# Token-major projections with 512 (in the first mixer 416) weight columns to a matmul, over four PSUM banks

## The chip, the cores and the metric

The kernel runs on one core of a Trainium2 chip. The metric is the device time of one execution in microseconds (us). It computes in float32; its large products are made of three matmuls each, on float32 values split into two halves of a narrower format (float32r).

## The reference

The input is a sequence of 512 tokens of width 1024 and a memory of 256 tokens. A first block has two layers (mixer, attention to the memory, squared-ReLU MLP); a second block has two hybrid layers with a context of 256 tokens. What the change touches are the projections whose result is wanted with tokens on the partitions:

```python
# first mixer: 512 columns for pooling, then latents of queries (256), keys and values (128), rotary keys (32)
u = h @ w_in_e[e]
b = mla_mixer(u[..., o1:o2], u[..., o2:o3], u[..., o3:], ...)
# second mixer: 16 heads of 64
qkv = (h @ w_qkv_o[o]).reshape(B, S, 3, NA_HEADS, NA_HEAD_DIM)
q = rms_norm(qkv[:, :, 0], na_q_g[o])
k = rms_norm(qkv[:, :, 1], na_k_g[o])
c = neighbourhood_attention(q, k, qkv[:, :, 2], na_rpb[o])
...
# hybrid layers: both for the 512 latents and the 256 tokens of context
# parts: ret q, k, v, gate (512 each), gla q, k (256 each), gla v, gate (512 each), two gate ranks of 16
lat = jnp.split(h @ w_in, offsets, axis=-1)
r = bidirectional_scan(retention_inputs(lat, True), ...)   # 4 heads, values of 128
g = bidirectional_scan(gla_inputs(lat), ...)               # 4 heads, values of 128
ret = from_heads(head_layernorm(r)) * jax.nn.silu(parts[3])
gla = from_heads(rmsnorm(g, gla_norm_g)) * jax.nn.silu(parts[7])
return jnp.concatenate([ret, gla], axis=-1) @ w_out
```

The second hybrid layer needs no output of the context, and so has no gates for it.

## The kernel before, in words

Activations lie feature-major in SBUF, 128 features by 512 tokens to a tile, as pairs `hi`, `lo`. Weights come from HBM in chunks of 512 KB on the SyncE queue (SP); `wload` (lines 227 to 244) casts a chunk to `whi` on ACT (line 241) and subtracts for `wlo` on DVE (line 242). All matmuls are issued on line 159 (`mat`), three to a product (`mat3`: hi by hi, hi by lo, lo by hi), and all transposes on line 171.

Most products are feature-major (`linear`): weights are the stationary operand, and 512 tokens stream by. Some are token-major (`linear_tm`, line 298): 128 tokens are the stationary operand and the weight columns stream by, 256 of them here. The result of 128 tokens by 256 columns is half of a PSUM bank, so a bank holds two token tiles (`per = 2`); 512 tokens need two banks and the context's 256 tokens one. An `evac` function, called once a bank at the product's end, copies the bank to SBUF on ACT.

There are eight banks in four sets: three `mm` for large products, three `pt` for transposes, scores and small products, one `po` for attention outputs, and one `bank` for streams that run beside the main one (the memory's keys and values, the modulation vectors). A bank that is given back can be written again when its last reader has read it.

The program is written by streams (generators). `run` (line 208) always steps the first stream whose operands should be there, by a clock that sums the length of the matmuls written so far; a stream yields how long its operands take or a condition. `take` and `give` (lines 174 and 181) count the banks that a stream holds over several steps. So each engine has a fixed queue, in which the pieces of many streams alternate, and the evacuations are written with `high_priority(200)`, which moves them forward in their engine's order.

The token-major products are: in the first mixer the latents, 256 and 160 columns after one another (`evac_c`, line 619: copies with a scale on ACT, lines 626 and 628, and squares); in the second mixer, for each of four groups of four heads, queries, keys and values of 256 columns each (`project`, line 873; `tm` is a copy of two token tiles, line 885, that is then normalized); in the hybrid layers `values` and `gates` (lines 1192 and 1203) with two products of 256 columns each, for keys "g" (gated heads) and "r" (retention heads). `values` copies a bank to `v` on ACT (line 1196). `gates` copies it to `gate_in` (line 1207), and then makes x sigmoid(x) of it: Abs, Exp, Ln, a DVE step, Exp on ACT, and a product on GpSimd (lines 1208 to 1213).

Beside these run the heads. A gated head (`gla`, line 1369) begins with a small matmul of its gates (tiles `gup` and `dd` or `dup` into `pt`), then a chain over ACT and DVE: Abs, Exp, Ln (lines 1375 to 1377, into `gb`), a scan and sums on DVE (`gc`, `tot`), Exp into `et` and `gb`, Exp into `ei` and `gc` (lines 1389 to 1397), then transposes of `gb` (to `ke`) and products of `gc` and `ei`. Two heads of a kind are under way at a time. `finish` (line 1269) normalizes a head's output and multiplies the gate. In the second mixer a `unit` (line 934) is the attention of two heads for 128 queries: scores in `pt`, Exp into `P` (line 957), two transposes, a copy `PT` (lines 969 and 972), products into `po`. In a hybrid layer the order of the projections is: gate ranks, gla keys, values "g", gla queries, ret keys, values "r", ret queries, gates "g", gates "r"; the products of the output follow.

Of the kernel before, what the change touches and what calls it, by code (L numbers as in the profile page):

```python
# [14 lines left out]
ALU = mybir.AluOpType  # L15
# [40 lines left out]
class Half:  # L56
    """a half of the tokens of a list of pairs of tiles, which may grow"""
# [24 lines left out]
class Net:  # L82
# [21 lines left out]
    # ---- storage  # L104
# [50 lines left out]
    # ---- tensor engine  # L155
# [17 lines left out]
    # ---- banks that a stream holds over several of its steps  # L173
# [52 lines left out]
    # ---- weights: a chunk of up to 1024 columns as an exact sum of two float32r tiles  # L226
    def wload(self, src, a, b, cut=1):
        nc = self.nc
        if self.side:
# [68 lines left out]
    def linear_tm(self, w, k0, kn, c0, cn, xs, ntok, evac, cut=1):  # L298
        """Token-major: 128 tokens on partitions; evac(i, tile of tokens i and features c0...)."""
# [4 lines left out]
        yield from self.take("mm", n // per)  # L304
        ps = [self.mm((128, per, cn)) for _ in range(n // per)]
        for kb in range(0, nk, kc):
            if len(xs) < kb + kc:
                yield lambda: len(xs) >= kb + kc
            hi, lo = self.wload(w[k0 + kb * 128:k0 + (kb + kc) * 128, c0:c0 + cn], kc, cn, cut if kb == 0 else 1)
# [5 lines left out]
            if kb + kc == nk:  # L315
# [3 lines left out]
                self.give("mm", n // per)  # L319
# [19 lines left out]
    def rows(self, r, n, copy=True):  # L339
        """a value of every token (tokens on partitions, column i for tile i), on all partitions"""  # L340
# [12 lines left out]
    def sq_add(self, st, x, w=T, half=None):  # L353
        """adds x * x to the running tile in the list st, or to a half of it"""
# [22 lines left out]
    def pair(self, w, nm=("hi", "lo")):  # L377
        """room for the two halves of w columns"""
# [12 lines left out]
    def split(self, x, g=None, w=T, rows=128, pair=None):  # L391
        """x (times a column g) as an exact sum of two float32r tiles"""
# [10 lines left out]
    # ---- residual stream  # L403
# [35 lines left out]
    # ---- keys and values of the memory  # L439
    def memory(self):  # L440
# [29 lines left out]
        for s in range(4):  # L470
# [6 lines left out]
            yield from self.linear_tm(A["w_mem_kv"], 0, D, D + s * 256, 256, h, NMEM, evac_v)  # L477
# [76 lines left out]
    # ---- squared-ReLU MLP of the first block  # L554
# [32 lines left out]
    # ---- first mixer: pooling and latent attention  # L587
    def mixer0(self):
# [30 lines left out]
        def evac_c(parts, dst):  # L619
            def f(q, p):  # L620
                w = parts[-1][1]
                c = self.t2(nm="c", w=2 * w).rearrange("p (i c) -> p i c", i=2)
                junk = self.t2(nm="junk", w=w)
                for ii in range(2):
                    i = q * 2 + ii
# [1095 lines left out]
```

## Time and profile before

| | us |
|---|---|
| median of 3 runs | 3344.96 (3344.82 to 3346.26) |
| profiled execution, span from first to last instruction | 3351.3 |
| TensorE (PE) busy | 3268.7, 98% |
| DVE busy | 1784.2, 53% |
| ACT busy | 1204.7, 36% |
| GpSimd (POOL) busy | 207.9, 6% |

The profile page gives one execution. Its span is the only time that it has for that execution, and it is 6.3 us over the median of the runs. PE is TensorE's matmuls, PEld its weight loads, which overlap them. The granted clock is the share of TensorE's full speed that it was given; its mean over the span is 0.986. In a row of the trace, `out<-in` are the program's tiles without their numbers, and what stands in brackets at its end is the idle time of the engine before it and what ended it.

The stages follow one another like this: first mixer and memory to about 190 us, modulation, memory attention and MLP to 880, second mixer to about 1133, its output, memory attention and MLP to 1633, hybrid layer 0 to 2080 and its MLP to 2600, hybrid layer 1 to 2990 and its MLP to the end.

### The profile page before, as it was taken

What the parts mean: (1) busy time and instruction counts of PE and PEld (TensorE: products, weight loads), DVE (VectorE), ACT (ScalarE), POOL (GpSimd) and SP (SyncE); (2) the same over time, 40 slices, a digit from 0 to 9 for tenths busy, and PEclk for the clock granted to TensorE, in tenths of its full rate; (3) what the DMA queues carried; (4) which work ended last, traced back from release to release, by engine and by line L of the source; (5) the groups of instructions that cost most, each with busy time, mean ns of one, the idle gap of its engine ahead of it and who ended that gap; (6) DMA issues with size and microseconds to landing.
All of it is one profiled execution on the core that took longest, in us unless ns stands there. A gap on an engine that the chain in (4) does not pass through costs nothing.

```text
span 3351.3 us, 45020 instructions
## 1 busy us (share of the span) xinstructions
PE 3268.7 (98%) x17942; PEld 2675.4 (80%) x17942; DVE 1784.2 (53%) x3208; ACT 1204.7 (36%) x2157; POOL 207.9 (6%) x257
## 2 busy tenths in 40 slices
PE   8999999999999999999999999999999989899998
PEld 8745448888988778888888987888888879788887
DVE  6853126444555646444776587333334755774444
ACT  5732224222444443222553354221322533433323
POOL 0100000000011100000011212000000011200000
PEclk9999999999999999999999999999999999899999
DMA  5356542332322123333442321222221433123332
GB/s 154 119 165 213 190 149 89 98 97 95 117 60 85 63 67 94 96 99 95 135 121 76 89 83 59 68 63 63 63 63 59 122 89 88 51 64 98 97 94 76
DMA packets 301858, 323.99 MB, mean 97 GB/s; under 512 B 18832, under 2 KB 270608, under 8 KB 301648
## 3 DMA queue, kind: packets, MB, share of 16 engines
q1 hardware_dynamic: 296656, 315.22, 30.9%
q10 hardware_dynamic: 4992, 5.90, 0.6%
q8 instruction: 141, 2.31, 0.3%
q14 instruction: 69, 0.57, 0.1%
HBM read 310.05 MB, written 2.10 MB: 93 GB/s over the span
## 4 chain that ended last, share of the span: by engine, by line
PE 93%; DVE 4%; ACT 1%; DMA 1%; issue 1%; SPq 0%; ACTq 0%; DVEq 0%
PE mm L159 77%; PE pt L159 6%; PE po L159 4%; PE bank L1023 3%; PE pt L171 1%; PE bank L159 1%; DMA raw<-in_w_mem_kv 1%; DVE wlo L242 1%; PE mm L171 0%; DVE S L1444 0%; DVE ht L1057 0%; ACT whi L241 0%; DVE sq L360 0%; DVE o L1289 0%; DMA raw<-in_w_in_e 0%
## 5 line engine op out<-in xcount | busy, mean ns | idle before, releaser
L242 DVE TENSOR_TENSOR wlo<-raw,whi 128x1024 fp32r<-128x1024 f32 (+2 forms) x503 | 598.1, 1190 | 747.5 <-ACT whi L241 724.6
L241 ACT CAST whi<-raw 128x1024 fp32r<-128x1024 f32 (+2 forms) x503 | 504.4, 1005 | 1248.4 <-PE mm L159 1094.4
L159 PE MATMUL mm<-hi,whi 128*128 128x512 f32 (+2 forms) x2768 | 887.1, 358 | 15.4 <-DVE cx L1124 6.1
L159 PE MATMUL mm<-hi,wlo 128*128 128x512 f32 (+2 forms) x2288 | 842.2, 369 | 0.0
L159 PE MATMUL mm<-lo,whi 128*128 128x512 f32 (+2 forms) x1808 | 707.7, 392 | 1.7 <-DVE lo L1062 1.6
L159 PEld LDWEIGHTS mm<-hi,whi 128*128 128x128 f32 (+1 forms) x2768 | 493.9, 190 | 111.3 <-issue 25.0
L159 PEld LDWEIGHTS mm<-hi,wlo 128*128 128x128 f32 (+1 forms) x2288 | 433.4, 189 | 85.8 <-issue 17.0
L159 PE MATMUL mm<-ahi,whi 128*128 128x512 f32 (+1 forms) x1552 | 489.7, 352 | 0.0
L159 PE MATMUL mm<-ahi,wlo 128*128 128x512 f32 (+1 forms) x1296 | 471.8, 366 | 0.0
L159 PEld LDWEIGHTS mm<-lo,whi 128*128 128x128 f32 (+1 forms) x1808 | 340.8, 188 | 87.4 <-issue 17.5
L159 PE MATMUL mm<-alo,whi 128*128 128x512 f32 (+1 forms) x1040 | 399.6, 386 | 0.0
L159 PE MATMUL mm<-whi,hi 128*128 128x256 f32 (+2 forms) x1392 | 367.5, 291 | 17.4 <-ACT v L1196 7.6
L159 PE MATMUL mm<-wlo,hi 128*128 128x256 f32 (+2 forms) x1200 | 346.3, 289 | 2.1 <-DVE wlo L242 2.1
L159 PEld LDWEIGHTS mm<-ahi,whi 128*128 128x128 f32 x1552 | 277.4, 189 | 40.8
L159 PE MATMUL mm<-whi,lo 128*128 128x256 f32 (+2 forms) x1008 | 289.4, 289 | 0.6 <-DVE lo L400 0.6
L159 PEld LDWEIGHTS mm<-whi,hi 128*128 128x128 f32 x1392 | 258.3, 195 | 25.3 <-ACT v L1196 7.8
L159 PEld LDWEIGHTS mm<-ahi,wlo 128*128 128x128 f32 x1296 | 244.4, 189 | 39.4
L159 PEld LDWEIGHTS mm<-wlo,hi 128*128 128x128 f32 x1200 | 234.4, 196 | 10.4 <-issue 6.4
L159 PEld LDWEIGHTS mm<-alo,whi 128*128 128x128 f32 x1040 | 195.5, 188 | 38.3
L159 PEld LDWEIGHTS mm<-whi,lo 128*128 128x128 f32 x1008 | 195.9, 195 | 5.5 <-issue 4.8
L1124 DVE SCALAR_TENSOR_TENSOR x<-mm,mod,x 128x512 f32<-128x512 f32 (+1 forms) x102 | 72.2, 717 | 99.5 <-PE mm L159 99.2
L1023 PE MATMUL bank<-ada,sil 128*32 128x512 f32 x384 | 122.4, 602 | 0.9 <-DMA ada<-in_ada_w 0.9
(320 smaller groups left out, 3254.4 us busy)
## 6 DMA issues: line engine op xcount, KB each, us to landing
raw<-in_w_ff SPq DMA_DIRECT2D x128, 512.0 KB, 3.6
raw<-in_w_mlp SPq DMA_DIRECT2D x128, 512.0 KB, 3.6
raw<-in_w_in SPq DMA_DIRECT2D x98, 512.0 KB, 3.8
ada<-in_ada_w SPq DMA_DIRECT2D x192, 256.0 KB, 3.7
raw<-in_w_qkv SPq DMA_DIRECT2D x24, 512.0 KB, 3.6
raw<-in_w_out SPq DMA_DIRECT2D x24, 512.0 KB, 3.5
raw<-in_w_mem_kv SPq DMA_DIRECT2D x32, 256.0 KB, 3.8
raw<-in_w_mem_q SPq DMA_DIRECT2D x16, 512.0 KB, 3.5
```

The lines of the kernel that those rows point to most:

```text
L159: return self.nc.tensor.matmul(out, lhsT=lhsT, rhs=rhs, start=start, stop=stop, **k).ins
L171: self.nc.tensor.transpose(out, in_, self.ident)
L241: nc.scalar.copy(hi[:, v], raw[:, v])
L242: nc.vector.tensor_sub(lo[:, v], raw[:, v], f32(hi[:, v]))
L1023: nc.tensor.matmul(p[32 * g:32 * g + 32], lhsT=sil[:, k], rhs=w, start=(k == 0), stop=(k == KT - 1), tile_position=(0, 32 * g))
L1124: self.nc.vector.scalar_tensor_tensor(x, p, self.mod[l][:, 16 + 24 * j + m, st:st + 1], x, ALU.mult, ALU.add)
```

## The change

`linear_tm` takes any number of column slices; with more than 256 columns a token tile has a bank of its own (`per = 1`), so 512 tokens take three `mm` banks and a fourth, which is `po` in the first mixer and the single `bank` elsewhere. All are held until the product's end. `wload` gets a list of slices, with a DMA for each. Docstrings and comments are taken out as well, which moves the line numbers (the cast of a chunk from 241 to 246, the copy `v` from 1196 to 1209, the copy `gate_in` from 1207 to 1224, the gated head's Abs from 1375 to 1393 and `ei` from 1396 to 1414, the copy `tm` from 885 to 897).

```diff
     def wload(self, src, a, b, cut=1):
+        parts = src if isinstance(src, list) else [src]
...
-            nc.sync.dma_start(raw[:, sl(i, n // cut)].rearrange("p (a b) -> p a b", b=b),
-                              src[sl(i, a // cut * 128)].rearrange("(k p) c -> p k c", p=128))
+            to, at = raw[:, sl(i, n // cut)].rearrange("p (a b) -> p a b", b=b), 0
+            for part in parts:
+                w = part.shape[1]
+                nc.sync.dma_start(to[:, :, at:at + w], part[sl(i, a // cut * 128)].rearrange("(k p) c -> p k c", p=128))
+                at += w
...
-    def linear_tm(self, w, k0, kn, c0, cn, xs, ntok, evac, cut=1):
+    def linear_tm(self, w, k0, kn, cols, xs, ntok, evac, cut=1, fourth=None):
+        cols = cols if isinstance(cols, list) else [cols]
+        cn = sum(c for _, c in cols)
         nk = kn // 128
         kc = min(nk, 1 << ((T if self.side else WCH) // cn).bit_length() - 1)
         n = ntok // 128
         per = 2 if cn <= 256 else 1
-        yield from self.take("mm", n // per)
-        ps = [self.mm((128, per, cn)) for _ in range(n // per)]
+        held = min(3, n // per)
+        yield from self.take("mm", held)
+        if fourth == "po":
+            yield from self.take("po")
+        ps = [self.mm((128, per, cn)) for _ in range(held)]
+        if n // per > held:
+            ps.append((self.po if fourth == "po" else self.bank)((128, per, cn)))
...
-            first = self.linear_tm(W, 0, D, 512, 256, h, T, evac_c([(0, 256, 256, 0)], cs), 2)
+            first = self.linear_tm(W, 0, D, (512, 416), h, T, evac_c, 2, "po")
...
-            yield from self.linear_tm(W, 0, D, 768, 160, h, T, evac_c([(0, 128, 128, 1), (128, 160, 96, 2)], kr))
...
-                yield from self.linear_tm(W, 0, D, c0 + g * 256, 256, h, T, evac)
+            yield from self.linear_tm(W, 0, D, [(g * 256, 256), (1024 + g * 256, 256)], h, T, evac)
...
         def values(key, c0):
-            for s in range(2):
-                def evac(q, p):
-                    t = self.t2(nm="v")
-                    nc.scalar.copy(t, p.rearrange("p i c -> p (i c)"))
...
-                yield from self.linear_tm(W, 0, D, c0 + 256 * s, 256, h, w, evac)
+            made = {}
+
+            def evac(i, p):
+                q, ii = divmod(i, 2)
+                for s in range(2):
+                    if ii == 0:
+                        made[s] = self.t2(nm="v")
+                    nc.scalar.copy(made[s][:, sl(ii, 256)], p[:, 0, sl(s, 256)])
...
+            yield from self.linear_tm(W, 0, D, (c0, 512), h, w, evac)
```

`gates` is changed like `values`: one product, two copies of 128 by 256 for each token tile, and the chain from Abs on once for two token tiles and two heads, as before. In the first mixer `evac_c` copies 256 and 160 columns of a token tile to two tiles. In the second mixer a `tm` tile now holds queries and keys of one token tile where it held one of them for two. The values of the second mixer and the memory's products stay at 256 columns or less. A chunk of 512 columns is two slices of k where it was four. On PE the program has 13831 rows of order where it had 15347.

Three places where the queues differ follow; a row is line, operation, tiles out and in, and size. Layer 0, ACT, end of the latent gates "r", before: two gated heads' chains (`gb_16713`, `gb_16740`) and then the copy of a bank of the first half of the columns (`mm_16764`).

```order
L1390 ACTIVATE gb_16713<-gb_16713 128x512
L1396 ACTIVATE ei_16730<-gc_16714 128x512
L1375 ACTIVATE gb_16740<-pt_16737,vecs 128x512
L241 CAST whi_17188<-raw_17187 128x1024
L1397 ACTIVATE gc_16714<-gc_16714 128x512
L1376 ACTIVATE gb_16740<-gb_16740 128x512
L1377 ACTIVATE gb_16740<-gb_16740,one 128x512
L1389 ACTIVATE et_16749<-tot_16748 128x8
L1390 ACTIVATE gb_16740<-gb_16740 128x512
L1396 ACTIVATE ei_16757<-gc_16741 128x512
L1207 COPY gate_in_16874<-mm_16764 128x512
```

After, at the same place:

```order
L1408 ACTIVATE gb_15837<-gb_15837 128x512
L1414 ACTIVATE ei_15854<-gc_15838 128x512
L1393 ACTIVATE gb_15864<-pt_15861,vecs 128x512
L1415 ACTIVATE gc_15838<-gc_15838 128x512
L1394 ACTIVATE gb_15864<-gb_15864 128x512
L1395 ACTIVATE gb_15864<-gb_15864,one 128x512
L1407 ACTIVATE et_15873<-tot_15872 128x8
L1408 ACTIVATE gb_15864<-gb_15864 128x512
L1414 ACTIVATE ei_15881<-gc_15865 128x512
L1224 COPY gate_in_15948<-mm_15744 128x256
L1224 COPY gate_in_15951<-mm_15744 128x256
L1224 COPY gate_in_15948<-mm_15745 128x256
```

The copies of all four banks of the one product of 512 columns now stand behind the second `ei`. On PE, before, where the second head's transposes of `gb_16740` are, matmuls of the other half of the gates (`mm_16987`) stand around them:

```order
L159 MATMUL mm_16987<-whi_16989,lo_13599 128x256
L159 MATMUL mm_16987<-whi_16989,hi_13604 128x256
L159 MATMUL mm_16987<-wlo_16990,hi_13604 128x256
L171 MATMUL pt_16911<-ident,gb_16740 128x128 x4
L159 MATMUL mm_16987<-whi_16989,lo_13605 128x256
L159 MATMUL mm_16987<-whi_16989,hi_13610 128x256
L159 MATMUL mm_16987<-wlo_16990,hi_13610 128x256
L159 MATMUL mm_16987<-whi_16989,lo_13611 128x256
L159 MATMUL mm_16987<-whi_17107,hi_13616 128x256
L159 MATMUL pt_16918<-gc_16741,ei_16757 128x128 x4
```

After, the last head's gate matmul reads `gup`, four matmuls of the product follow (in the fourth bank, `bank_15747`), and then small products of the heads up to the first matmul of the output for the context (`mm_16082`), which takes the bank of `mm_15744`:

```order
L159 MATMUL bank_15747<-whi_15919,hi_13148 128x512
L159 MATMUL bank_15747<-wlo_15920,hi_13148 128x512
L159 MATMUL pt_15861<-dd_14234,gup 128x512
L159 MATMUL bank_15747<-whi_15919,lo_13149 128x512
L159 MATMUL bank_15747<-whi_15919,hi_13154 128x512
L159 MATMUL bank_15747<-wlo_15920,hi_13154 128x512
L159 MATMUL bank_15747<-whi_15919,lo_13155 128x512
L171 MATMUL pt_15988<-ident,gb_15837 128x128 x4
L159 MATMUL pt_15995<-gc_15838,ei_15854 128x128 x4
L159 MATMUL pt_16001<-gc_15838,ei_15854 128x128 x4
L159 MATMUL po_16148<-v_14618,gp_15859 128x128
L171 MATMUL pt_16007<-ident,gb_15864 128x128 x4
L159 MATMUL mm_16082<-hi_14102,whi_16084 128x256 x2
```

In layer 1 the end of the gates has the same order. The second mixer, third group, PE, before: matmuls of keys (`mm_8584`) alternate with the transposes of units (`P`).

```order
L159 MATMUL mm_8584<-whi_8664,lo_7123 128x256
L159 MATMUL mm_8584<-whi_8664,hi_7036 128x256
L159 MATMUL mm_8584<-wlo_8665,hi_7036 128x256
L159 MATMUL mm_8584<-whi_8664,lo_7037 128x256
L171 MATMUL pt_8326<-ident,P_8234 128x128
L171 MATMUL pt_8326<-ident,P_8234 64x128
L171 MATMUL pt_8326<-ident,P_8234 128x128
L171 MATMUL pt_8326<-ident,P_8234 64x128
L171 MATMUL pt_8346<-ident,P_8267 128x128
L171 MATMUL pt_8346<-ident,P_8267 64x128
L171 MATMUL pt_8346<-ident,P_8267 128x128
L171 MATMUL pt_8346<-ident,P_8267 64x128
```

After, the q,k product ends in `bank_8087`, and the rows behind it are those of units alone (39 rows, to the first matmul of the values):

```order
L159 MATMUL bank_8087<-whi_8275,hi_7026 128x512
L159 MATMUL bank_8087<-wlo_8276,hi_7026 128x512
L159 MATMUL bank_8087<-whi_8275,lo_7027 128x512
L159 MATMUL pt_8023<-kT_7920,qT_7913 128x256
L171 MATMUL pt_8031<-ident,P_7927 128x128 x4
L171 MATMUL pt_8038<-ident,P_7946 128x128
L171 MATMUL pt_8038<-ident,P_7946 64x128
L171 MATMUL pt_8038<-ident,P_7946 128x128
L171 MATMUL pt_8038<-ident,P_7946 64x128
L171 MATMUL pt_8058<-ident,P_7979 128x128
L171 MATMUL pt_8058<-ident,P_7979 64x128
L171 MATMUL pt_8058<-ident,P_7979 128x128
```

Layer 1, ACT, latent values "g", before: copies of the first half's banks (`mm_23219`, `mm_23220`) behind the second gated head's `ei`.

```order
L1389 ACTIVATE et_23208<-tot_23207 128x8
L1390 ACTIVATE gb_23199<-gb_23199 128x512
L1396 ACTIVATE ei_23216<-gc_23200 128x512
L1196 COPY v_23329<-mm_23219 128x512
L1196 COPY v_23331<-mm_23220 128x512
L1196 COPY v_23443<-mm_23333 128x512
```

After, the copies of all 512 columns stand there:

```order
L1407 ACTIVATE et_22060<-tot_22059 128x8
L1408 ACTIVATE gb_22051<-gb_22051 128x512
L1414 ACTIVATE ei_22068<-gc_22052 128x512
L1209 COPY v_22219<-mm_22095 128x256
L1209 COPY v_22221<-mm_22095 128x256
L1209 COPY v_22219<-mm_22096 128x256
L1209 COPY v_22221<-mm_22096 128x256
L1209 COPY v_22225<-mm_22097 128x256
```

Nothing of that product is left behind these copies, where 48 matmuls of the second half were.

## Rows read from the trace of the kernel before

**Rows 1.** page part 1: engine, busy us (share), instructions
```profile
PE 3268.7 (98%) x17942; PEld 2675.4 (80%) x17942; DVE 1784.2 (53%) x3208; ACT 1204.7 (36%) x2157; POOL 207.9 (6%) x257
```

**Rows 2.** page part 4: share of the chain that ended last
```profile
PE 93%; DVE 4%; ACT 1%; DMA 1%; issue 1%; SPq 0%; ACTq 0%; DVEq 0%
PE mm L159 77%; PE pt L159 6%; PE po L159 4%; PE bank L1023 3%; PE pt L171 1%; PE bank L159 1%; DMA raw<-in_w_mem_kv 1%; DVE wlo L242 1%; PE mm L171 0%; DVE S L1444 0%; DVE ht L1057 0%; ACT whi L241 0%; DVE sq L360 0%; DVE o L1289 0%; DMA raw<-in_w_in_e 0%
```

**Rows 3.** windows: stretch us, length, PE busy (instructions), granted clock, DMA share, GB/s
```profile
879.00:914.00 35.00, 35.00 (x294) 1.00 0.35 99
990.00:995.00 5.00, 5.00 (x27) 0.50 0.01 3
995.00:1000.00 5.00, 5.00 (x24) 0.50 0.00 0
1103.00:1133.00 30.00, 26.09 (x181) 1.00 0.02 6
1775.00:1780.00 5.00, 1.90 (x11) 0.82 0.00 0
2710.00:2715.00 5.00, 0.66 (x4) 0.85 0.00 0
2715.00:2720.00 5.00, 1.76 (x8) 0.50 0.02 3
2720.00:2725.00 5.00, 5.00 (x30) 0.63 0.00 0
```

**Rows 4.** chain of waits, longest pieces: start us, us, what
```profile
537.97 340.84 PE mm L159 x1528
...
879.59 34.18 PE mm L159 x284
...
1783.67 6.41 PE mm L159 x48
```

**Rows 5.** timeline of PE: start us, us, engine, line, operation, tiles
```profile
36.73 0.28 PE L159 MATMUL mm<-wlo,hi 128*128 128x160 f32 x1
...
38.74 0.28 PE L159 MATMUL mm<-wlo,hi 128*128 128x160 f32 x1
```

**Rows 6.** timeline of ACT, layer 1, two gated heads, then the values' copies
```profile
2700.61 0.69 ACT L1375 ACTIVATE gb<-pt,vecs 128x512 f32<-128x512 f32 x1 [5.58 <-PE pt L159]
...
2709.15 0.61 ACT L1396 ACTIVATE ei<-gc 128x512 f32<-128x512 f32 x1
...
2709.67 0.67 ACT L1375 ACTIVATE gb<-pt,vecs 128x512 f32<-128x512 f32 x1
...
2717.11 0.61 ACT L1396 ACTIVATE ei<-gc 128x512 f32<-128x512 f32 x1
...
2717.62 0.56 ACT L1196 COPY v<-mm 128x512 f32<-128x512 f32 x1
```

**Rows 7.** waits of PE: us in total, times, longest
```profile
PE mm L159 <- ACT v L1196: 7.6, 1, 7.6
...
PE mm L159 <- ACT whi L241: 6.2, 1, 6.2
```

**Rows 8.** lines by form, ACT reading banks: busy us, mean ns, idle before
```profile
L1545 ACT ACTIVATE relu<-mm 128x256 f32<-128x256 f32 x36 | 11.8, 381 | 35.6 <-PE mm L159 35.6
...
L1196 ACT COPY v<-mm 128x512 f32<-128x512 f32 x24 | 13.6, 582 | 24.4 <-PE mm L159 24.4
```

**Rows 9.** timeline of ACT, layer 0, end of a gated head
```profile
1946.71 0.61 ACT L1396 ACTIVATE ei<-gc 128x512 f32<-128x512 f32 x1
1947.23 0.56 ACT L1207 COPY gate_in<-mm 128x512 f32<-128x512 f32 x1
```

**Rows 10.** timeline of PE, layer 1, behind the values' copies
```profile
2718.24 0.58 PE L159 MATMUL mm<-whi,hi 128*128 128x256 f32 x1 [7.56 <-ACT v L1196]
...
2723.53 0.37 PE L159 MATMUL mm<-whi,hi 128*128 128x256 f32 x1
...
2726.50 0.40 PE L159 MATMUL mm<-hi,whi 128*128 128x512 f32 x1
```

More of the change, by code (lines that the diff above doesn't have):

```diff
@@ L308, in linear_tm @@
                 yield lambda: len(xs) >= kb + kc
-            hi, lo = self.wload(w[k0 + kb * 128:k0 + (kb + kc) * 128, c0:c0 + cn], kc, cn, cut if kb == 0 else 1)
+            r = slice(k0 + kb * 128, k0 + (kb + kc) * 128)
+            hi, lo = self.wload([w[r, a:a + b] for a, b in cols], kc, cn, cut if kb == 0 else 1)
             for i in range(n):
@@ L318, in linear_tm @@
                         evac(q, p)
-                self.give("mm", n // per)
+                self.give("mm", held)
+                if fourth == "po":
+                    self.give("po")
             yield 0.0
@@ L475, in evac_v @@
                 self.mv.append([t[:, sl(i, 256)] for i in range(2)])
-            yield from self.linear_tm(A["w_mem_kv"], 0, D, D + s * 256, 256, h, NMEM, evac_v)
+            yield from self.linear_tm(A["w_mem_kv"], 0, D, (D + s * 256, 256), h, NMEM, evac_v)
         ss = self.rsqrt(ss)
@@ L717, in evac_q @@
                     rq[s, q] = self.rsqrt(self.affine(r, 1.0, 96 * EPS, 4))
-                yield from self.linear_tm(A["w_uq"], 0, 256, s * 192, 192, lat[0:2], T, evac_q)
+                yield from self.linear_tm(A["w_uq"], 0, 256, (s * 192, 192), lat[0:2], T, evac_q)
                 def evac_k(q, p):
@@ L745, in evac_k @@
                     k_tm[s, q] = k4
-                yield from self.linear_tm(A["w_ukv"], 0, 128, s * 256, 256, lat[2:3], T, evac_k)
+                yield from self.linear_tm(A["w_ukv"], 0, 128, (s * 256, 256), lat[2:3], T, evac_k)
         def heads_t(s):
@@ L881, in project @@
                 o.tab += [t[:, sl(0, 256)], t[:, sl(1, 256)]]
-            for nm, c0 in (("q", 0), ("k", 1024)):
-                def evac(q, p):
-                    t, sq = self.t2(nm="tm"), self.t2(nm="sq")
-                    nc.scalar.copy(t.rearrange("p (i h) -> p i h", i=2), p)
-                    nc.scalar.activation(sq, t, AF.Square)
-                    r = self.tiny(8, "nr")
-                    nc.vector.tensor_reduce(r, sq.rearrange("p (h c) -> p h c", c=64), AX.X, ALU.add)
-                    for ii in range(2):
-                        i = 2 * q + ii
-                        nc.vector.tensor_scalar(r[:, sl(ii, 4)], r[:, sl(ii, 4)], 1.0 / 64, em[:, i:i + 1],
-                                                ALU.mult, ALU.add)
-                    r = self.rsqrt(r)
-                    v = t.rearrange("p (h c) -> p h c", c=64)
-                    nc.vector.tensor_mul(v, v, r.unsqueeze(2).to_broadcast((128, 8, 64)))
-                    o.tm[nm, q] = t
-                yield from self.linear_tm(W, 0, D, c0 + g * 256, 256, h, T, evac)
+            def evac(i, p):
+                t, sq = self.t2(nm="tm"), self.t2(nm="sq")
+                nc.scalar.copy(t, p[:, 0])
+                nc.scalar.activation(sq, t, AF.Square)
+                r = self.tiny(8, "nr")
+                nc.vector.tensor_reduce(r, sq.rearrange("p (h c) -> p h c", c=64), AX.X, ALU.add)
+                nc.vector.tensor_scalar(r, r, 1.0 / 64, em[:, i:i + 1], ALU.mult, ALU.add)
+                r = self.rsqrt(r)
+                v = t.rearrange("p (h c) -> p h c", c=64)
+                nc.vector.tensor_mul(v, v, r.unsqueeze(2).to_broadcast((128, 8, 64)))
+                o.tm[i] = t
+            yield from self.linear_tm(W, 0, D, [(g * 256, 256), (1024 + g * 256, 256)], h, T, evac)
             def evac_v(q, p):
@@ L905, in evac_v @@
                     o.v[i] = t[:, sl(ii, 256)]
-            yield from self.linear_tm(W, 0, D, 2048 + g * 256, 256, h, T, evac_v)
+            yield from self.linear_tm(W, 0, D, (2048 + g * 256, 256), h, T, evac_v)
             for jj in range(2):
@@ L923, in transposes @@
                     for i in range(4):
-                        self.tr(p[:, sl(i)], o.tm[nm, i // 2][:, sl(i % 2, 256)][:, sl(j)])
+                        self.tr(p[:, sl(i)], o.tm[i][:, sl("qk".index(nm), 256)][:, sl(j)])
                     t = self.t2(nm=nm + "T")
@@ L1192, in values, with evac @@
         def values(key, c0):
-            for s in range(2):
-                def evac(q, p):
-                    t = self.t2(nm="v")
-                    nc.scalar.copy(t, p.rearrange("p i c -> p (i c)"))
-                    for ii in range(2):
-                        for hh in range(2):
-                            V[key, 2 * s + hh, 2 * q + ii] = t[:, sl(ii, 256)][:, sl(hh)]
-                yield from self.linear_tm(W, 0, D, c0 + 256 * s, 256, h, w, evac)
-        def gates(key, c0):
-            for s in range(2):
-                def evac(q, p):
-                    u, t = self.t2(nm="gate_in"), self.t2(nm="gate")
-                    nc.scalar.copy(u, p.rearrange("p i c -> p (i c)"))
+            made = {}
+            def evac(i, p):
+                q, ii = divmod(i, 2)
+                for s in range(2):
+                    if ii == 0:
+                        made[s] = self.t2(nm="v")
+                    nc.scalar.copy(made[s][:, sl(ii, 256)], p[:, 0, sl(s, 256)])
+                    for hh in range(2):
+                        V[key, 2 * s + hh, i] = made[s][:, sl(ii, 256)][:, sl(hh)]
+            yield from self.linear_tm(W, 0, D, (c0, 512), h, w, evac)
+        def gates(key, c0):
+            made = {}
+            def evac(i, p):
+                q, ii = divmod(i, 2)
+                for s in range(2):
+                    if ii == 0:
+                        made[s] = self.t2(nm="gate_in"), self.t2(nm="gate")
+                    u, t = made[s]
+                    nc.scalar.copy(u[:, sl(ii, 256)], p[:, 0, sl(s, 256)])
+                    for hh in range(2):
+                        G[key, 2 * s + hh, i] = t[:, sl(ii, 256)][:, sl(hh)]
+                    if ii == 0:
+                        continue
                     nc.scalar.activation(t, u, AF.Abs)
@@ L1213, in evac @@
                     nc.gpsimd.tensor_mul(t, t, u)
-                    for ii in range(2):
-                        for hh in range(2):
-                            G[key, 2 * s + hh, 2 * q + ii] = t[:, sl(ii, 256)][:, sl(hh)]
-                yield from self.linear_tm(W, 0, D, c0 + 256 * s, 256, h, w, evac)
+            yield from self.linear_tm(W, 0, D, (c0, 512), h, w, evac)
         def narrow(nm):
```

21 lines of the change are left out of this document (8 added, 13 removed).

## The prediction

> **What bounds the kernel now.** I read the page's first part, then the chain of waits, then the waits by line, and last the timeline and the windows of the places that the change touches. TensorE works for 3268.7 of 3351.3 us [rows 1], so all its idle time together is 82.6 us; no other engine is over 53%. The chain of work that ended last lies on PE for 93%, the matmuls of line 159 alone for 77% [rows 2]. So a matmul less is time less, unless it stood in a stretch in which PE waits anyway; and a new wait of PE is time more, twice over, since after a wait the granted clock drops: in the five microseconds around 2710 to 2715 PE works for 0.66 us, and in the two windows behind it the clock is 0.50 and 0.63 of full speed [rows 3]. 0.50 is the 1.2 GHz level, 1.00 the 2.4 GHz level.
>
> **What a wide product saves.** The chain piece at 879.59 us, the first projections of the second mixer, is 284 matmuls of 256 columns in 34.18 us, 0.1204 us each; the piece at 537.97 is 1528 matmuls of 512 columns in 340.84 us, 0.2231 each [rows 4]. Two of 256 become one of 512: 2 x 0.1204 - 0.2231 = 0.0177 us a pair. I take 0.017, since neither piece is pure to the last matmul. Pairs: one product is 8 slices of k x 3 partial products x its token tiles (4 for the 512 tokens, 2 for the context). Second mixer: 4 head groups x 96 = 384. Hybrid layer 0: values and gates, two kinds each, 4 x 96 for the latents and 4 x 48 for the context = 576. Layer 1 has no context gates: 480. So 6.5 + 9.8 + 8.2 = 24.5 us. First mixer: 96 pairs of 256 and 160 columns become 96 of 416. 160 columns take 2.01 us for 18, 0.112 each [rows 5]; 416 has no row, and between the two rows of 256 and 512 it is 0.120 + 160/256 x 0.103 = 0.184 (an estimate). 96 x (0.120 + 0.112 - 0.184) = 4.6 us. Together 29 us of PE time. It was all on PE's path, since in these stretches PE is busy but for the waits below.
>
> The token-major 512-wide matmul itself has no row: the 1528 have weights as the stationary side. Bounds: as priced, 29 us; or no cheaper per column than 256 (0.241), 0. I take the first, because in both kinds each matmul has a stationary tile of its own (PE's weight loads are as many as its matmuls [rows 1]).
>
> The Trainium skill (TensorE: Matmul & The Clock Gate, "Wait — 56ns, not 53.3ns?") has back-to-back matmuls at full clock cost their columns at 2.4 GHz and about 2.5 ns on top. By that rule a pair saves 2.5 ns and the 1536 pairs under 4 us, which speaks against the change. The trace disagrees: the 256 wide ones stand 0.1204 us apart and not 0.109 [rows 4], so the row decides.
>
> **What it adds: ends of products.** Before, a product of 512 tokens held two of the three mm banks, and the next product began in the third while ACT copied. Now it holds three and the fourth, so the first matmul of the next product waits for ACT's first copies. These copies are not first in ACT's queue: in layer 0 the order puts the gate copies behind the whole chain of two gated heads, Abs to ei, and so in layer 1; the same for the values. The trace has this once: in layer 1 the chain's first Abs starts at 2700.61, the first ei 8.5 us later, the second chain runs from 2709.67 to 2717.11, and only then the copies of v, at 2717.62 [rows 6]. PE waited 7.6 us for them, the longest wait of a matmul on ACT [rows 7]. The copies themselves are short: a 512 wide one 0.58 us, a 256 wide one about 0.38 [rows 8], so eight for four are 3.0 against 2.3 us; a bank is free after its two, 0.8 us.
>
> Place by place, beyond the saved matmuls:
> - *Layer 0, gates of the retention heads.* Before, the copies came right behind ei too (1946.71, 1947.23 [rows 9]), but these were of the first two heads, and PE had the 96 matmuls of the other half to do. Now, by the order, four matmuls are left when the last gated head's gate matmul (the one into pt that reads gup) is issued. Its chain takes 7.4 us [rows 6] and 0.5 to 1 to PE and the copies; PE has four matmuls (0.9), transposes and small products of some 2 to 3 us: 5 us idle. Behind it half clock: 5 us at 0.5 to 0.6 [rows 3] cost 2 to 2.5; in layer 1 the first 24 matmuls behind the wait took 5.3 us and the next 24 3.0 [rows 10], 2.3 us more. And all four heads' gates now come at the end, so the finish of the first heads is 2 us later. Sum +9.5.
> - *Layer 0, latent values.* Here PE already waited (1775 to 1780: 1.90 of 5 busy) and then did the remaining 48 matmuls in 6.41 us, 0.134 each [rows 3, 4]. The copies come about when they did, but nothing of the product is left behind them: 6.4 less some 1.3 for eight copies and 1.6 that I counted as saved: -3.5.
> - *Layer 1, latent values.* The wait grows, since by the order 20 matmuls (4.5 us) stand behind the chain's start where some 50 of half the width stood: some 12 us instead of 7.6. The 48 matmuls behind it, 8.3 us from 2718.24 to 2726.50 [rows 10], go. The chain starts 5.7 us later (by the order 76 matmuls of 0.223 in front, where 94 of 0.120 stood), and so do the copies. 5.7 - 8.3 + 1.6 (counted as saved) = -1.
> - *Layer 1, gates.* As in layer 0, +8. There the scan of the last heads is behind the eight copies and the gate chain, 7 us later on its path; part comes back, as gate copies are no longer in the last heads' chain, and about 12 more output matmuls are done before: +1. Sum of layer 1: +8.
> - *Second mixer.* In the third head group the eight attention units in flight stand alone, from the end of the q,k product to the v product, where matmuls stood between them; smaller clusters stand behind the second and the fourth. Units with little else run 26.09 of 30 us at 1103 to 1133; there was such a spot before, at half clock from 990 to 1000 [rows 3]. Three spots of some 1.5 us idle and a microsecond or two of lost clock, less what the one of before cost: +5, from 0 to 12.
> - *First mixer.* The first step has two slices of k instead of four, and two 512 KB transfers more stand on SP ahead of nothing that is late; both transfers at the start are a little smaller. +0.5, from -3 to +4.
> - *Else nothing.* The weights are as many bytes (2 KB runs where 1 KB were); DMA's share is 0.35 in a dense stretch of these projections [rows 3], and PE's waits for weights are single ones of 6.2 us at most [rows 7], which hides what the order of chunks does. The gate chain's activations, DVE and POOL steps are the same in number.
>
> Sum: 0.5 + 5 + (9.5 - 3.5) + 8 = 19.5 us of new waits against 29 saved: -9.5. The profiled execution spans 3351.3, 6.3 over the median of the runs, with nothing in it that the runs lack as far as the rows show; 3351.3 - 9.5 = 3341.8 in its terms, 3335.5 in the runs'. I say 3336.
>
> **Rivals.**
> 1. *Full credit.* PE stays the bound and the waits are covered by other streams: 3345 - 29 = 3316. For it: PE busy for 97.5%, and the retention heads and the context's output product as filler. Against it: the order has none at the two ends of gates, where the copies of all four banks follow ei.
> 2. *The saving is just eaten.* Waits of 25 to 32 us, 3340 to 3348. For it: clusters in the second mixer and later scans in both layers, of which I took the middle.
> 3. *Slower: the held fourth bank.* Each of the four ends of latent values and gates beside the gated heads costs what the rows show for one [rows 3, 7], 7.6 + 2.5 = 10 us, and the three spots of the second mixer 3.5 us each: 40 + 10.5 = 50.5 less 10 that the values of layer 1 pay already = 40.5, less 29: 3356. It decides from 36 us of added waits on, 5.1 us at each of seven places. Against it: at the two value products the matmuls behind the wait go with it.
> 4. *Wide is not cheaper* (the lower bound of the saving): 3345 + 19.5 = 3364. The chain's rows speak against it [rows 4]. The rule of the Trainium skill (TensorE: Matmul & The Clock Gate, the section cited above) would come near this rival, since it leaves 4 us of the saving.
>
> **How the numbers follow.** Faster or slower by 0.2% (6.7 us) is about what these runs tell from no change: under 3338.3, over 3351.6. My forecast holds 0.47 (waits of 12 to 28 us, 3328 to 3344, of it 0.42 under the bound and 0.05 within), full credit 0.14, eaten 0.21, slower by the fourth bank 0.15, wide not cheaper 0.03. Faster 0.56, same 0.26, slower 0.18. The range leaves out a tenth on either side: 3320 to 3354; the likeliest case alone 3328 to 3344.
>
> **What would show it.** Chain pieces of wide token-major matmuls near 0.223 us each, and 1536 fewer matmuls; if they are near 0.24, the price is wrong. In the waits by line, PE behind ACT's gate copy at two places of some 5 us, and one behind the copy of v of over 10 us in layer 1; windows at 0.50 behind each. In the second mixer idle of a few us around the third group. If PE's idle time grows by under 8 us in all, the full credit was right; if by more than 30, the slower rival.

## The result: slower by 0.6%

| | us |
|---|---|
| before, median of 5 runs | 3344.96 (3343.56 to 3348.15) |
| changed kernel, median of 5 runs | 3367.16 (3366.73 to 3370.19) |
| ratio | 1.0062, 95% interval 1.005 to 1.0074 |
| profiled execution of the changed kernel | 3370.19, span 3368.4 |

I forecast 3336, in 3320 to 3354, with 0.18 for slower; it came out 22 us slower. The profiled execution of the changed kernel lies 3 us over its median, that of before (span 3351.3 and 1.8 us around it) 8 us; so the two profiles stand only 17 us apart, and where a few us matter I go by runs.

The page's first part and the two lines of the chain of the changed kernel [rows 1, 2]:

```profile
PE 3269.1 (97%) x16406; PEld 2599.5 (77%) x16406; DVE 1770.4 (53%) x3192; ACT 1206.6 (36%) x2201; POOL 200.5 (6%) x257
...
PE 93%; DVE 4%; ACT 1%; issue 1%; DMA 1%; DVEq 0%; SPq 0%; ACTq 0%
PE mm L159 75%; PE pt L159 6%; PE po L159 4%; PE bank L1032 4%; PE bank L159 3%; PE pt L171 2%; DVE S L1462 1%; DVE wlo L247 0%; PE mm L171 0%; DVE ht L1066 0%; DMA gl<-in_mla_g_nope 0%; DVE sq L377 0%; ACT whi L246 0%; DMA mem<-in_mem 0%; DVE gc L1398 0%
```

PE has 1536 matmuls fewer (17942 before) and yet is busy as long as before (3268.7): what the wide products saved came back as matmuls at half clock, and its idle time grew from 82.6 to 99.3 us. Summed over windows of 2.5 us of the whole span, the time lost to the clock (busy time by one minus the granted clock) went from 35.7 to 56.0 us; so the work itself, counted at full clock, shrank from 3232.9 to 3213.1, by 20 us, while idle time and clock took 37 us more. The windows of three stages, first of the kernel before, then of the changed kernel (stretch, length, PE busy, granted clock, DMA share, GB/s; the second mixer up to the MLP behind it, then hybrid layer 0, then layer 1, from the end of one MLP to the start of the next):

```profile
878.00:1292.00 414.00, 409.12 (x2538) 0.98 0.24 75
1633.47:2079.57 446.10, 426.39 (x2926) 0.98 0.33 95
2600.18:2990.19 390.01, 359.30 (x2340) 0.93 0.30 83
```

```profile
874.00:1285.00 411.00, 405.48 (x2194) 0.99 0.25 77
1625.86:2085.57 459.71, 427.61 (x2349) 0.94 0.32 92
2606.16:3007.28 401.12, 363.85 (x1862) 0.90 0.28 81
```

Layer 0 is 13.6 us longer and layer 1 11.1, with more idle time and a lower clock, in spite of 577 and 478 matmuls fewer. Summed in the same way, idle time went from 19.7 to 32.1 us in layer 0 and from 30.7 to 37.3 in layer 1; time lost to the clock from 7.4 to 20.2 and from 19.5 to 29.3. The loss lies at the end of the layers: from the last copies of the values "r" to the end, layer 0 took 211 us before and 224 now. There, on PE behind the last gates of layer 0 (x2 in a row is two instructions told as one):

```profile
1934.93 0.39 PE L159 MATMUL mm<-whi,lo 128*128 128x512 f32 x1
...
1937.65 0.39 PE L159 MATMUL mm<-whi,lo 128*128 128x512 f32 x1
...
1938.42 1.12 PE L159 MATMUL pt<-dd,gup 32*128 32x512 f32 x2
...
1940.28 0.40 PE L159 MATMUL bank<-whi,lo 128*128 128x512 f32 x1
1944.85 1.09 PE L171 MATMUL pt<-ident,gb 128*128 128x128 f32 x4 [4.17 <-DVE gb L1411]
1946.11 3.06 PE L159 MATMUL pt<-gc,ei 64*128 64x128 f32 x16 [0.17 <-DVE gc L1418]
1951.63 0.79 PE L159 MATMUL po<-v,gp 128*128 128x128 f32 x2 [2.46 <-DVE gp L1433]
...
1953.15 0.78 PE L159 MATMUL mm<-hi,whi 128*128 128x256 f32 x2
```

```profile
1935.00:1940.00 5.00, 5.00 (x20) 1.00 0.34 105
1940.00:1945.00 5.00, 0.83 (x4) 0.68 0.20 62
1945.00:1950.00 5.00, 4.00 (x20) 0.50 0.16 56
1950.00:1955.00 5.00, 3.37 (x14) 0.50 0.00 0
```

The last matmul of the gates is at 1940.28, the next dense product begins at 1953.15: of these 12.9 us 6.8 are idle and the rest small products, with the clock at 0.50, the 1.2 GHz level, in the windows from 1945 to 1955. This is the place that the prediction priced at 5 us idle and 2 to 2.5 of clock. But it was not the copies that PE waited for longest: it was the third gated head's own chain (`gb`, `gp`), whose gate matmul starts 13 us ahead of the product's last matmul here (1927.32) and 34 us ahead before (1924.76 and 1958.60). The wait for the values' copies in layer 1 is as long as it was [rows 7]:

```profile
PE pt L171 <- DVE gb L1411: 8.3, 2, 4.2
PE mm L159 <- ACT v L1209: 7.6, 1, 7.6
PE pt L171 <- ACT gb L1408: 6.7, 1, 6.7
```

The price of a matmul did not quite hold: from 1934.93 to 1937.65 they are 0.227 us apart, where 0.223 was taken from [rows 4]. The kernel before has the same 0.227. Its piece of 1528 matmuls runs on into the second mixer, whose matmuls of 256 columns begin at 872.41, and so its mean is too low. Two windows of before that hold matmuls of 512 columns alone and of 256 alone:

```profile
540.00:870.00 330.00, 330.00 (x1458) 1.00 0.31 98
880.00:913.00 33.00, 33.00 (x277) 1.00 0.34 97
```

That is 0.227 and 0.120 us each, start to start, and a pair saves 2 x 0.120 - 0.227 = 0.013 us, not 0.017.

### The profile page after: what moved, and what is told of

It is laid out like the page before. It is cut to its first block, busy times and chain, and to the rows that moved or that the text cites. A ratio compares the mean times of both kernels' runs of the same rounds, so it can differ in the third digit from the quotient of the medians.

```text
span 3368.4 us, 41986 instructions
## 1 busy us (share of the span) xinstructions
PE 3269.1 (97%) x16406; PEld 2599.5 (77%) x16406; DVE 1770.4 (53%) x3192; ACT 1206.6 (36%) x2201; POOL 200.5 (6%) x257
## 4 chain that ended last, share of the span: by engine, by line
PE 93%; DVE 4%; ACT 1%; issue 1%; DMA 1%; DVEq 0%; SPq 0%; ACTq 0%
PE mm L159 75%; PE pt L159 6%; PE po L159 4%; PE bank L1032 4%; PE bank L159 3%; PE pt L171 2%; DVE S L1462 1%; DVE wlo L247 0%; PE mm L171 0%; DVE ht L1066 0%; DMA gl<-in_mla_g_nope 0%; DVE sq L377 0%; ACT whi L246 0%; DMA mem<-in_mem 0%; DVE gc L1398 0%
## 5 line engine op out<-in xcount | busy, mean ns | idle before, releaser
L247 DVE TENSOR_TENSOR wlo<-raw,whi 128x1024 fp32r<-128x1024 f32 (+4 forms) x503 | 591.3, 1177 | 763.7 <-ACT whi L246 730.9
L246 ACT CAST whi<-raw 128x1024 fp32r<-128x1024 f32 (+4 forms) x503 | 505.9, 1007 | 1279.7 <-PE mm L159 1048.0
L159 PE MATMUL mm<-whi,hi 128*128 128x512 f32 (+3 forms) x680 | 237.2, 373 | 9.2 <-ACT whi L246 5.9
L159 PE MATMUL mm<-wlo,hi 128*128 128x512 f32 (+3 forms) x584 | 213.5, 366 | 2.0 <-DVE wlo L247 2.0
L159 PE MATMUL mm<-whi,lo 128*128 128x512 f32 (+3 forms) x488 | 173.4, 359 | 0.0
L159 PEld LDWEIGHTS mm<-whi,hi 128*128 128x128 f32 x680 | 130.6, 193 | 33.8 <-ACT whi L246 6.2
L159 PEld LDWEIGHTS mm<-wlo,hi 128*128 128x128 f32 x584 | 113.3, 194 | 19.5 <-issue 2.5
L159 PEld LDWEIGHTS mm<-whi,lo 128*128 128x128 f32 x488 | 94.0, 193 | 15.1 <-issue 3.6
```

Source lines behind the costliest of these rows:

```text
L159: return self.nc.tensor.matmul(out, lhsT=lhsT, rhs=rhs, start=start, stop=stop, **k).ins
L246: nc.scalar.copy(hi[:, v], raw[:, v])
L247: nc.vector.tensor_sub(lo[:, v], raw[:, v], f32(hi[:, v]))
```

## Experiments

Four theories. A landmark in the texts below is the time at which a trace reaches a named point, such as the last copy of a product. Theory 1: the loss is made at the end of the last gates of a hybrid layer. Theory 2: every wide product costs, since it holds its banks until ACT has copied them. Theory 3: the order is mixed up as a whole and nothing adds up. Theory 4 came out of the first four runs. All kernels here are the changed one but for what their diff shows (cut to the lines that tell; `gates_two` is `gates` in two products of 256 columns); all ratios are to before, in runs on the same chip.

**Which of the wide products cost.** e1 takes values and gates of the hybrid layers back to two products of 256 columns, e2 the gates, e3 the values, e5 only the last projection, the latents' gates "r":

```diff
 # e2_values (e1_mixers: values as well; e3_gates: values alone)
-            yield from self.linear_tm(W, 0, D, (c0, 512), h, w, evac)
+            for s in range(2):
...
+                yield from self.linear_tm(W, 0, D, (c0 + 256 * s, 256), h, w, evac)
...
 # e5_last
-                yield from gates("r", 1536)
+                yield from (gates_two if w == T else gates)("r", 1536)
```

> Both mixers of the first block with wide products as in the changed kernel, values and gates of the hybrid layers two by 256 columns as before. Theory 1 (what was lost is lost in the hybrid layers, at the end of the last gates): the traces' landmark behind the second mixer is 7.6 us earlier, so 3337 us, 0.998 of before. Theory 2 (every wide product that holds its banks costs some us): the mixers hold them too, so 3345 to 3350. Theory 3 (the order is mixed up as a whole, no part adds up): anything, not 3337.

> As the changed kernel, with the gates of the hybrid layers in two products of 256 columns as before; values stay at 512. Theory 1: the values' part of the landmarks is about nought (layer 0: 6 us won up to the latent values g, 8 lost before values r; layer 1 won 3, lost 3), so as e1, 3337 +- 3. Theory 2: half of the 25 us that the two hybrid layers lost, 3350.

> As the changed kernel, with the values of the hybrid layers in two products of 256 columns as before; gates stay at 512. Theory 1: nearly all the loss is left, e1 plus 22 to 25, 3360. Theory 2: half of it, 3350.

> As the changed kernel, but the last projection of each hybrid layer alone, the latents' gates of the retention heads, in two products of 256 columns as before. Theory 1: from the landmark of the gates g to the layer's end the changed kernel lost 13.6 us in layer 0 and 11.5 in layer 1; these 25 come back: 3342, and in the trace no wait of over 3 us behind the last gates. Theory 2: two of eight wide products fewer, 3360.

| | ratio, 95% interval | median us (before beside it 3348.2) |
|---|---|---|
| e1_mixers | 0.9991, 0.9982 to 1.0001 | 3345.72 |
| e2_values | 0.9964, 0.9952 to 0.9976 | 3336.96 |
| e3_gates | 1.0072, 1.006 to 1.0084 | 3373.99 |
| e5_last | 1.004, 1.0028 to 1.0052 | 3361.66 |

The mixers give 3 us and not 7.6. Values give 9 more (0.9991 to 0.9964), with some 5 us either way; their whole saving, 576 pairs by 0.013, is 7.7. Beside wide gates they give 3 (1.0072 in e3 to 1.0062), also with some 6 either way. Gates cost 0.0098 of 3347, 33 us, with values wide, and 27 without (e3 over e1). By the numbers alone neither theory wins. On the base of the forecasts (the ratio by 3345) e1 is 3342, between theory 1's 3337 and theory 2's 3345 to 3350; e2 is 3333, nearer to theory 1's 3337; e3 is 3369, above both. With the last gates split 1.004 is left, 3358, near theory 2's 3360: of the 33 us only 7 come back, where theory 1 wanted 25. But theory 2 as it was stated is out too, as values hold the same banks and cost nothing. Something in the other gates was still unnamed.

**What late gates do.** The trace of layer 1 names it. Before, the last copy of the gates "g" of heads 0 and 1, the last copy of those of heads 2 and 3, and then the gate matmuls (`gup`) of heads 2 and 3:

```profile
2844.69 0.57 ACT L1207 COPY gate_in<-mm 128x512 f32<-128x512 f32 x1
...
2854.73 0.58 ACT L1207 COPY gate_in<-mm 128x512 f32<-128x512 f32 x1 [0.21 <-PE mm L159]
```

```profile
2855.43 1.12 PE L159 MATMUL pt<-dd,gup 32*128 32x512 f32 x2
2862.20 1.12 PE L159 MATMUL pt<-dd,gup 32*128 32x512 f32 x2
```

The changed kernel, the last copy of the gates "g", and the same two:

```profile
2860.27 0.66 ACT L1224 COPY gate_in<-bank 128x256 f32<-128x256 f32 x2
```

```profile
2871.12 1.12 PE L159 MATMUL pt<-dd,gup 32*128 32x512 f32 x2
2882.22 1.12 PE L159 MATMUL pt<-dd,gup 32*128 32x512 f32 x2
```

Head 2 starts 10.7 us behind the last copy of the gates of heads 0 and 1 before, and 10.9 in the changed kernel: two heads are under way at a time, head 0 can't finish without its gate, and head 2 starts when it has. But before, that copy is the first half's, half a product ahead of the end (the second half's last copy is at 2854.73); now it is the end itself. So heads 2 and 3 start 10.9 and 22 us behind the end of the gates "g" and not 0.7 and 7.5 (the traces of layer 0 have the same distances), and what runs beside them, the gates "r" of 21 us, is nearly over. Theory 4: it is this lateness that costs, not width and not banks. e6 makes heads 0 and 1 late without any of the rest (it exchanges the two halves of the columns):

```diff
 # e6_swap, on e2_values
-            for s in range(2):
+            for s in ((1, 0) if key == "g" and w == T else (0, 1)):
...
 # e13_gwide, on e2_values: wide gates "g" of the latents alone; e8_rwide: of "r" alone; e9_ctx: both of the context
-                yield from gates_two("g", 3072)
+                yield from (gates if w == T else gates_two)("g", 3072)
...
 # e10_mixer0, on e2_values: evac_c and the first mixer's two products as before
```

> As e2_values (gates in two products of 256), but in the latents' gates of the gated heads the halves change places: the columns of heads 2 and 3 come first, those of heads 0 and 1 second. No product is wider, no bank is held longer, no matmul is added. Theory 4 (the first two gated heads get their gates half a product later, so they finish later, so the next two start later and have no dense matmuls left to run beside): gup of the third head moves from 1 to 11 us behind the end of these gates, and most of what wide gates cost comes back: 3337 + 15 to 25 = 3352 to 3362. Theory 2 (it is the banks, held to the end and freed behind the gated heads' chain): nothing changes, 3337.

> As e2_values, with only the latents' gates of the retention heads, the last projection of a hybrid layer, 512 wide with all four banks held. It is the other half of e5_last. Theory 4: the gated heads get their gates as early as in e2_values, and the end of the product costs some 3 us in a layer less 1.6 saved: 3337 + 0 to 7. Theory 2 (a held fourth bank at the layer's end): 3337 + 20.

> As e2_values, with the two gate products of the context in layer 0 512 wide as well (two banks held, of three). Theory 4 and theory 2 alike: 96 pairs of matmuls at 0.017 us are 1.6 us saved; the heads of the context get their gates up to 5 us later, with the latents' projections behind them to cover it: 3337 - 2 to + 3.

> As e2_values, but the first mixer's latents as before, 256 and then 160 columns. The MLP of the first layer began at 537 to 538 us in each profile, before or after, so the wide latents gave nothing: as e2_values, 3337 +- 2. If they had given their 4 us: 3341.

> As e2_values, with only the latents' gates of the gated heads 512 wide. Theory 4 (late gates of the first two heads): the exchange of halves alone cost 7.6 us in layer 0 and 5.3 in layer 1 of the traces; wide, the gates of heads 0 and 1 come as late and all four sets of the chain queue on ACT at once, which makes gup of the fourth head 4 us later still, less 1.6 saved in each layer: e2_values plus 13 to 20, 3350 to 3357. If the costs of the parts don't add up (theory 3): well outside of that.

| | ratio, 95% interval | over e2_values, us | median us (before beside it) |
|---|---|---|---|
| e6_swap | 1.0007, 0.9998 to 1.0016 | 14 | 3349.55 (3346.87) |
| e13_gwide | 1.0018, 1.0009 to 1.0027 | 18 | 3351.04 (3347.12) |
| e9_ctx | 0.9992, 0.9983 to 1.0001 | 9 | 3342.19 (3346.87) |
| e8_rwide | 0.9981, 0.9972 to 0.999 | 6 | 3341.11 (3346.87) |
| e10_mixer0 | 0.997, 0.9959 to 0.9981 | 2 | 3338.30 (3346.87) |

The third column is the difference of the ratios by 3347; each has some 5 us of uncertainty either way, as two ratios enter it. In e6 the gate copies of heads 0 and 1 end the product at 2844.04 and `gup` follows 12.3 us later:

```profile
2844.04 0.59 ACT L1219 COPY gate_in<-mm 128x512 f32<-128x512 f32 x1 [0.21 <-PE mm L159]
```

```profile
2856.33 1.12 PE L159 MATMUL pt<-dd,gup 32*128 32x512 f32 x2
2862.00 1.12 PE L159 MATMUL pt<-dd,gup 32*128 32x512 f32 x2
```

In e2, with the same kernel but for the exchange, the two `gup` stand at 2840.72 and 2847.49, 0.7 and 7.5 us behind the last copy of these gates (2840.01), as before. Not a matmul is added and no bank is held longer, and the exchange alone costs 14 us (15 to 25 were expected), of the 18 that the wide gates "g" cost. That shows theory 4 for the largest of the three parts, against theory 2, which wanted nothing. Why the lateness costs, that little dense work is left beside heads 2 and 3, is read from the traces; no run puts work there. The three parts, 18, 9 and 6, sum to the 33 of all, so theory 3 finds no support; with 5 us of uncertainty in each part a few us of interplay would not show.

e9 missed: I expected nothing of the context's gates, since the latents' projections stand behind them. In its trace the context's heads 2 and 3 start later, and the latents' first two gated heads start close together, 6.9 us apart where e2 (the first two rows) has 12.9:

```profile
1750.94 1.12 PE L159 MATMUL pt<-dd,gup 32*128 32x512 f32 x2
1763.85 1.12 PE L159 MATMUL pt<-dd,gup 32*128 32x512 f32 x2
```

```profile
1754.10 1.12 PE L159 MATMUL pt<-dd,gup 32*128 32x512 f32 x2
1760.99 1.12 PE L159 MATMUL pt<-dd,gup 32*128 32x512 f32 x2
```

PE then waits once for 6.7 us, ahead of the copies of the latent values "g":

```profile
1774.04 1.51 PE L171 MATMUL pt<-ident,o 128*128 128x128 f32 x6 [6.69 <-ACT gb L1425]
```

The changed kernel has the same wait (`gb L1408` above), and e2 none over 2 us there. That it is the whole of the 9 us is not shown, and no run makes the context's gates late without making them wide. e8 is what the prediction thought to be the main cost: gates "r" at the end, 6 us for both layers. e10 lies 2 us over e2, between its two forecasts (nothing, and 4 us): what the wide latents of the first mixer give is too small for these runs.

**Two remedies that did not help.**

```diff
 # e12_order, on the changed kernel: Abs ... product on GpSimd, after all eight copies
+                for s in range(2):
+                    for q in range(n // 2):
+                        u, t = made[s, q]
...
 # e11_early, on e2_values, latents
+                    yield from gates("g", 3072)
                 yield from heads("rq", 0, 128 ** -0.5)
-                yield from gates("g", 3072)
```

> As the changed kernel, every product as wide, but the gate chain (Abs to the product on GpSimd) is written for heads 0 and 1 first, then for heads 2 and 3, after all eight copies, where it was by token tiles. Heads 0 and 1 get their gates some 3 to 4 us earlier than in the changed kernel, still some 7 later than with two products. Theory 4: a third of the 11 us of lateness is taken away, so 3 to 8 us of the time: 3360 to 3364. Theory 2 (banks): the copies and the banks are as they were, 3367.

> As e2_values, but the latents' gates of the gated heads are projected before the retention heads' queries, not behind them, so gup of the third and fourth head come one product of 21 us earlier. Theory 4 (dense matmuls left to run beside the last two gated heads): less idle behind the last gates, 3325 to 3337. Against it: the retention heads' queries come later, and their end may take the place: 3337 to 3350.

e12 came out at 1.0077 (1.0063 to 1.009; 3371.53 us), not faster than the changed kernel. It did not do what it was made for: from the last copy to `gup` it is 12.8 us and not 7:

```profile
2858.67 0.63 ACT L1224 COPY gate_in<-bank 128x256 f32<-128x256 f32 x2
```

```profile
2871.50 1.12 PE L159 MATMUL pt<-dd,gup 32*128 32x512 f32 x2
```

ACT and GpSimd had the same work to do between the two, and the copies now came first; that this is the reason is not shown. So the run says nothing against theory 4, and nothing for it. e11 came out at 0.9977 (0.9968 to 0.9987; 3338.46 us), 4 us over e2 with 5 either way: the gain over e2 that theory 4 had forecast did not come. The gated heads do start earlier, but the wait moves to the retention heads, whose queries are late now, and to the gates "r":

```profile
1930.43 1.88 PE L159 MATMUL pt<-qk,qk 128*128 128x128 f32 x8 [4.17 <-DVE kd L1325]
...
1956.11 0.39 PE L159 MATMUL mm<-whi,hi 128*128 128x256 f32 x1 [1.60 <-ACT gate_in L1219]
```

The version that beats both kernels is e2_values: wide products in the mixers and for the values, the gates in two halves, 0.36% faster than before.

## Why the prediction was wrong

- *What a pair saves*: the right kind, a quarter too much. It is 0.013 us and not 0.017, since the piece of 1528 matmuls was not pure; 24.5 us of the sum become 19, and with the first mixer 29 become 23. Counted at full clock the trace has 20 us less work. The rule of the Trainium skill (TensorE: Matmul & The Clock Gate, "Wait — 56ns, not 53.3ns?") gives a fixed 2.5 ns for each matmul at 2.4 GHz; by it a pair would save 2.5 ns and the 576 pairs of the values 1.4 us, an estimate. The trace contradicts it for these matmuls: 13 ns a pair.
- *Second mixer*, forecast 6.5 saved and 5 given back: not contradicted. Both mixers together are 3 us faster in runs (interval 0 to 6). In the trace idle time is as before (5.5 us, 4.9), so the stretches of attention units alone hardly cost.
- *First mixer*, 4.6 saved and 0.5 given back: not seen, and not ruled out by the runs (2 us, with 5 either way). The first MLP begins at 537.97 us before, at 536.65 in e10, and between 535.5 and 538.9 in the kernels with wide latents. In the profiled execution of the changed kernel PE waits for the squares of a norm (`sq`) with the product begun, and then does the product at half clock; the matmuls behind 22.15 are 0.35 us apart and not 0.19:

```profile
17.82 0.34 PE L159 MATMUL po<-whi,hi 128*128 128x416 f32 x1
20.45 1.84 PE L159 MATMUL pt<-mean,sq 128*128 128x1 f32 x8 [2.29 <-DVE sq L377]
22.15 0.69 PE L159 MATMUL mm<-wlo,hi 128*128 128x416 f32 x1
...
26.81 0.40 PE L159 MATMUL mm<-wlo,hi 128*128 128x416 f32 x1
```

  That is this execution's. The stretch has a granted clock of 0.97 before, 0.93 in the changed kernel and 0.97 again in e2, which has the same wide latents:

```profile
10.00:60.00 50.00, 47.24 (x340) 0.97 0.55 164
```

```profile
10.00:60.00 50.00, 46.85 (x253) 0.93 0.54 161
```

```profile
10.00:60.00 50.00, 47.10 (x263) 0.97 0.53 165
```

- *Latent values*, waits that were to pay back 4.5 us beyond the saved matmuls: they paid back nothing that the runs show, but cost nothing.
- *Gates*: this is the step that failed. The forecast priced the end of the last product, the gates "r", with the copies behind `ei`: +9.5 and +8, of it 2 us because "all four heads' gates now come at the end, so the finish of the first heads is 2 us later". Those gates cost 6 us net in runs (e8), less than the 17.5 less 3 saved. The latents' gates "g", the product ahead of them, had no term at all, and cost 18 (e13). There the lateness was 10 us, half a product, and I did not follow it to the start of heads 2 and 3. The context's gates had no term either, and cost 9 (e9). All gates were to cost 17.5 less 8 saved, and cost 33 net.
- *Rival 3, the held fourth bank*, had the sign, and with 40.5 us of new waits nearly the size: in the traces idle time and lost clock grew by 37 us. But its reason was not the one: it charged values and gates alike. The sign that the forecast set for it, over 30 us more idle time on PE, did not come; idle time grew by 17 us, and more than half of the loss, 20 us, came as clock.

I had both facts in hand: the order showed `gup` of the last head four matmuls ahead of the product's end, and the kernel showed that `finish` waits for a head's gate. I priced the place where the queue had changed, and not the time at which its inputs came.

What is left open: from the profile of e2 to that of the changed kernel, the gates alone, idle time grows by 17.7 us and lost clock by 19.8, against 8 us less work; how the 33 us in runs divide is not known, as each is one execution. A kernel that fills the wait with other matmuls was not run.

## What to carry to other kernels

A product that is made wider hands over all its columns at its end. Before pricing the matmuls that it saves, measure one in a window that holds no other kind, and ask who waits for the first half of the columns, and follow that consumer to what it starts next: here the saving was under 3 us for the latents' gates "g" of both layers (192 pairs by 0.013), and the lateness 10 us in each, at a place with little dense left to run. For the values the saving was kept, as far as the runs can tell; that their consumers come late enough is the likely reason, and was not tested. An exchange of the two halves, one line, shows most of the cost without the wide product (e6).

## What the runs showed of the hardware

The same code took different times in different executions on a single core. From the start of the first MLP to that of the second, the kernels with the wide products of both mixers took 744 to 753 us, with the same instructions in it. The granted clock makes the 9 us between the two ends: e3_gates and e1_mixers, the second mixer, with the same 0.25 of DMA:

```profile
874.00:1281.00 407.00, 401.46 (x2188) 1.00 0.25 78
```

```profile
874.00:1290.00 416.00, 411.36 (x2191) 0.97 0.25 76
```

The same 15 us of the time axis in both, e3 first:

```profile
994.00:1009.00 15.00, 14.12 (x103) 1.00 0.01 2
```

```profile
994.00:1009.00 15.00, 15.00 (x62) 0.51 0.00 1
```

With the same instructions the clock stayed at 2.4 GHz in one execution and was for a part at 1.2 in the other, 9 us apart. So a single profile of this kernel can be off by some 8 us in 3350, as that of before is; the runs of e1 alone reach from 3338 to 3355. Differences of this size were settled by ratios of many runs.

At 2.4 GHz matmuls with a weight load of their own stood 0.120 us apart with 256 columns and 0.227 with 512. The 256 columns between them cost 0.107 us, which is 256 at 2.4 GHz, and 0.013 us is left with each matmul however wide of the two it is. 160 columns took 0.112 us [rows 5], so below 256 columns the price hardly falls.
